# An encoder layer in three float32r products: the low parts of weights written by ACT and an adding DMA instead of a subtraction on DVE

## The chip, the cores and the metric

The kernel runs on one core of one Trainium2 chip. The metric is the device time of one launch in microseconds (us); the median of the runs is given. Engines are named as the profile names them: PE (TensorE), DVE (VectorE), ACT (ScalarE), POOL (GpSimd) and SP (SyncE, which here only issues DMAs).

## The reference

One layer of a bidirectional encoder is applied with the same weights to two requests: a prompt of 512 tokens and a sample of 1024 tokens, with 1024 channels, all in float32. Shortened to one request:

```python
def encoder_layer(x, c, ...):
    sh1, sc1, gt1, sh2, sc2, gt2 = split(silu(c) @ w_ada + b_ada, 6)
    h = rms_norm(x, g_pre_mix) * (1 + sc1) + sh1
    xa, ya, xb, ga, gb = split(h @ w_in)          # 1024, 1024, 512, 1024, 1024 columns
    xa = depthwise_conv(xa, conv_w, conv_b)       # width 4
    y_a = ((rg_lru(xa, forward) + rg_lru(xa, backward)) * gelu(ya)) @ w_a_out
    y_b = fourier_mix(xb) @ w_b_out               # 2-D DFT over positions and channels of a group
    x = x + gt1 * rms_norm((sigmoid(ga) * y_a + sigmoid(gb) * y_b) @ w_o, g_post_mix)
    h = rms_norm(x, g_pre_ffn) * (1 + sc2) + sh2
    val, gate = split(depthwise_conv(h @ w_up, ffn_conv_w, ffn_conv_b))   # 2816 and 2816, width 3
    return x + gt2 * rms_norm((gelu(gate) * val) @ w_down, g_post_ffn)

y_prompt = encoder_layer(x_prompt, c_prompt, ...)
y_sample = encoder_layer(x_sample, c_sample, ...)
```

## The kernel before

**Three products for one.** PE multiplies float32r, a rounded float32. Each float32 operand w is therefore split into a high part hi = float32r(w) and a low part lo = w − hi, and a product is the sum of hi·hi, hi·lo and lo·hi, added up in PSUM. The functions `passes`, `fm_mm` and `km_mm` issue them; all their matmuls have the line L200, and the transposes have L203.

**Units of weights.** The weights are worked off in units. A unit is one tile `raw` of 128 x 1024 float32, 512 KB, which `load_unit` loads by a DMA on SP's queue (L123; there are RAW_BUFS = 3 such tiles). `prep_unit` splits it into the two halves of a tile `hl` (HL_BUFS = 4 such tiles). There are three kinds of split. For a unit with `on_act`, ACT writes the high part (L108, a copy that rounds) and DVE subtracts it from the raw tile into the low part (L111). For a unit without `on_act`, DVE does both. A mixed unit (`mix`, the weights w_b of the Fourier branch) is first put together from sums and differences by DVE. 196 units have `on_act`: the sample's first projections (24, with 16 more for ya of both requests), w_a in the two merges (16), w_o and w_down (90), and the up projection where it is done plainly (50). The sample's up projection is mostly done by blocks (`up_quads`, seven block products in place of eight); its units have `whole=False`, and `prep_unit` isn't called for them.

**Steps and their order.** The program is one list of steps. A step has a unit, the products `mm` that use it, and what follows (`post`). `emit` goes through the list in order and, ahead of the products of step i, emits the splits of the units up to AHEAD = 3 further on, and the raw loads up to RAW_BUFS units beyond these; other loads of a step (`loads`) are emitted LOAD_AHEAD = 5 steps ahead. The instructions of an engine, and the DMAs of a queue, run in the order in which they were emitted. Only SP issues DMAs in this kernel. A function put off by `defer` is emitted one or more steps later.

**The stages**, with the times at which they stand in the profiled execution: the lead-in and the prompt's first projections (0 to 190 us), its Fourier branch and ya (to 280), the prompt merge (280 to 328), the prompt's w_o (to 373), the sample's first projections, Fourier branch and merge (to 960) and w_o (to 1030), the prompt's up projection (to 1297), the prompt's w_down (to 1425), the sample's up projection (to 1864) and the sample's w_down (to 2107), then the tail. Three of them matter for what follows:

- In the prompt merge (`merge_steps`), units of w_b (mixed, their products shorter) and of w_a (`on_act`, products yh x hl) take turns.
- In the prompt's w_down (`rows_steps`: 24 products a step), ACT also normalizes the sample's rows for the next sub-layer, one row of 128 tokens a step (`norm_rows`): a square with a sum (L412), two small operations on POOL for the reciprocal root (L429, L430, in `rstd`), and one step later the scaling (L417). The transposes of these rows (L203) follow from 1341.75 us on, between the weight steps.
- In the sample's w_down (`rows_steps` with `fsrc`), the activations f were stored to DRAM by the up projection (`fs`). In the first eleven of its steps, two tiles `fq` of 512 KB per step are read back on SP's queue (L1033), beside the raw weights, and are split into `ah` and `al` by ACT (L108) and DVE (L111) in `pre`, ahead of the step's weights.

Of the kernel before, what the change touches and what calls it, by code (L numbers as in the profile page):

```python
# [12 lines left out]
AF = mybir.ActivationFunctionType  # L13
ALU = mybir.AluOpType
PSUM = bass.MemoryType.PSUM
# [56 lines left out]
class Enc:  # L72
# [13 lines left out]

# [1 line left out]
    def nm(self, s):  # L88
# [14 lines left out]

# [1 line left out]
    def split(self, hi, lo, src, act=False, keep=None):  # L105
# [7 lines left out]
    def split_all(self, pairs):  # L113
        """Splits out of PSUM: one engine's reads of a bank before the other's."""
        nc = self.nc
        for out, src in pairs:
            nc.scalar.activation(out=out[:, 0, :], in_=src, func=AF.Copy)
        for out, src in pairs:
            nc.vector.tensor_tensor(out=out[:, 1, :], in0=src, in1=out[:, 0, :].bitcast(F32), op=ALU.subtract)
# [5 lines left out]
    def prep_unit(self, u):  # L125
        hl = self.sb.tile([128, 2, u.cols], F32R, tag="hl", bufs=HL_BUFS, name=self.nm("hl"))
        u.hi, u.lo = hl[:, 0, :], hl[:, 1, :]
        src = u.raw
        if u.mix:
            nc = self.nc  # L130
            src = self.big([128, u.cols], name="wb")
# [4 lines left out]
        if u.mix:  # L136
# [3 lines left out]
            return  # L140
        self.split(u.hi, u.lo, src, act=u.on_act)

# [1 line left out]
    def defer(self, fn, d):  # L144
# [52 lines left out]

# [1 line left out]
    def mmul(self, *args, **kw):  # L199
# [27 lines left out]
    def fm_chunks(self, sq, ps, f, mirror=False):  # L227
        """Output columns and the operand's; a mirrored operand has the later half of the tokens back to front."""
        n = sq.n
        cols = [slice(0, 512), slice(n, n // 2, -1) if mirror else slice(512, 1024)]  # L230
        return [(ps[:, f, c * 512:(c + 1) * 512], cols[c]) for c in range(sq.chunks)]
# [15 lines left out]

# [1 line left out]
    def setup(self):  # L249
# [71 lines left out]
    def ada_steps(self, job):  # L321
        """One part of the conditioning: a row of its weights per partition, two dot products with each."""
        nc = self.nc
# [53 lines left out]

# [1 line left out]
    def fold_loads(self):  # L379
# [25 lines left out]

# [1 line left out]
    def norm_rows(self, x, later):  # L407
# [81 lines left out]

# [1 line left out]
    def lead_in(self, sq, src, jobs, hb, sizes):  # L491
# [150 lines left out]

# [1 line left out]
    def conv_a(self, sq, ps, g, box):  # L644
# [150 lines left out]

# [1 line left out]
    def pq_steps(self, sq, hb, pq):  # L797
# [108 lines left out]

# [1 line left out]
    def merge_steps(self, sq, yb, z, sig, mg):  # L908
# [84 lines left out]

# [1 line left out]
    def rows_steps(self, sq, table, act, gate, src, dst, last=False, fsrc=None):  # L995
# [106 lines left out]

# [1 line left out]
    def quad_sums(self, hb):  # L1104
        """Sums of the activations' blocks (halves of the channels by halves of the tokens), in two parts as they are."""
        nc = self.nc
# [38 lines left out]
    def up_quads(self, sq, hb, dst, plain):  # L1145
        """The widest product by blocks, seven products of blocks for two tiles of columns."""
        nc = self.nc
# [3 lines left out]
        def finish(g, ca, cb):  # L1151
            """Convolution, gelu and product, a little at a time."""
            box = {}
# [278 lines left out]

# [1 line left out]
def _dft(n):  # L1434
# [105 lines left out]
```

## Time and profile before

| what | value |
|---|---|
| time, median of 3 runs | 2117.44 us (2117.34 to 2117.49) |
| span of the profiled execution, first to last instruction | 2115.4 us |
| PE busy | 2096.1 us, 99% |
| PE weight loads, beside the matmuls | 1721.6 us, 81% |
| DVE busy | 1424.4 us, 67% |
| ACT busy | 915.9 us, 43% |
| POOL busy | 55.0 us, 3%, 124 instructions |
| DMA | 274.66 MB, mean 130 GB/s; queue of SP 37.1% of the 16 engines' span |
| mean granted TensorE clock | 0.999 |

For the profiled execution the profile gives its span; the time of a run is taken around the whole launch, and the median lies 2.0 us above this span. Busy time is that of the engine's instructions; waiting and issuing are not in it. The stretches between the times above can be read apart, with the busy time of each engine in each of them.

### The profile page before, as it was taken

What the parts mean: (1) busy time and instruction counts of PE and PEld (TensorE: products, weight loads), DVE (VectorE), ACT (ScalarE), POOL (GpSimd) and SP (SyncE); (2) the same over time, 40 slices, a digit from 0 to 9 for tenths busy, and PEclk for the clock granted to TensorE, in tenths of its full rate; (3) what the DMA queues carried; (4) which work ended last, traced back from release to release, by engine and by line L of the source; (5) the groups of instructions that cost most, each with busy time, mean ns of one, the idle gap of its engine ahead of it and who ended that gap; (6) DMA issues with size and microseconds to landing.
All of it is one profiled execution on the core that took longest, in us unless ns stands there. A gap on an engine that the chain in (4) does not pass through costs nothing.

```text
span 2115.4 us, 24826 instructions
## 1 busy us (share of the span) xinstructions
PE 2096.1 (99%) x9866; PEld 1721.6 (81%) x9866; DVE 1424.4 (67%) x1815; ACT 915.9 (43%) x1199; POOL 55.0 (3%) x124
## 2 busy tenths in 40 slices
PE   7999999999999999999999999999999999999998
PEld 6888888888888988888888888888888888888887
DVE  5787888667666734655676545649688887875553
ACT  2447355265464422144433335633344444455442
POOL 0000010000000000000100000000000000000000
PEclk9999999999999999999999999999999999999999
DMA  9343474332332413433453224332122222284422
GB/s 350 114 149 130 180 269 162 113 109 85 110 105 65 141 50 108 141 141 135 175 186 112 99 99 156 113 130 90 50 80 80 90 72 82 96 315 163 149 91 109
DMA packets 90803, 274.66 MB, mean 130 GB/s; under 512 B 8736, under 2 KB 26560, under 8 KB 90688
## 3 DMA queue, kind: packets, MB, share of 16 engines
q1 hardware_dynamic: 90688, 273.09, 37.1%
q8 instruction: 77, 1.26, 0.2%
q14 instruction: 38, 0.31, 0.1%
HBM read 234.22 MB, written 38.83 MB: 129 GB/s over the span
## 4 chain that ended last, share of the span: by engine, by line
PE 95%; ACT 2%; DVE 1%; DMA 1%; issue 0%; POOL 0%; SPq 0%; DVEq 0%; POOLq 0%; ACTq 0%
PE ps L200 94%; PE ps L203 1%; DMA x<-in_x_prompt_dram 0%; ACT xn L412 0%; ACT th L685 0%; DVE hl L111 0%; DMA x<-in_x_sample_dram 0%; DVE yb L964 0%; ACT th L695 0%; ACT ea L693 0%; POOL sm L430 0%; DVE th L716 0%; DVE th L721 0%; ACT xn L417 0%; DVE th L719 0%
## 5 line engine op out<-in xcount | busy, mean ns | idle before, releaser
L200 PE MATMUL ps<-hh,hl 128*128 128x512 f32 x2144 | 633.8, 395 | 0.0
L200 PEld LDWEIGHTS ps<-hh,hl 128*128 128x128 f32 x2144 | 403.7, 188 | 95.2 <-DVE hl L111 0.2
L200 PE MATMUL ps<-hl,ah 128*128 128x512 f32 x1440 | 452.2, 395 | 0.0
L200 PE MATMUL ps<-hl,hl 128*128 128x512 f32 (+1 forms) x1264 | 436.2, 378 | 0.0
L111 DVE TENSOR_TENSOR hl<-raw,hl 128x1024 fp32r<-128x1024 f32 (+2 forms) x244 | 293.8, 1206 | 163.3 <-ACT hl L108 160.9
L200 PE MATMUL ps<-hx,wq 128*128 128x512 f32 x1596 | 370.9, 394 | 0.0
L200 PEld LDWEIGHTS ps<-hx,wq 128*128 128x128 f32 x1596 | 299.6, 188 | 71.1 <-DVE wq L1222 0.2
L108 ACT ACTIVATE hl<-raw 128x1024 fp32r<-128x1024 f32 x196 | 205.6, 1054 | 270.8 <-PE ps L200 243.4
L200 PEld LDWEIGHTS ps<-hl,ah 128*128 128x128 f32 x1440 | 269.1, 188 | 61.5
L200 PE MATMUL ps<-hl,al 128*128 128x512 f32 x720 | 283.8, 394 | 0.0
L200 PEld LDWEIGHTS ps<-hl,hl 128*128 128x128 f32 x1264 | 238.3, 189 | 47.5
L200 PEld LDWEIGHTS ps<-hl,al 128*128 128x128 f32 x720 | 135.2, 188 | 31.8
L1318 DVE SCALAR_TENSOR_TENSOR cf<-ps,vec,cf 128x511 f32<-128x511 f32 (+1 forms) x100 | 75.2, 807 | 83.8 <-ACT cf L1310 83.6
L200 PE MATMUL ps<-yh,hl 128*128 128x512 f32 x384 | 111.9, 394 | 0.3 <-DVE hl L111 0.3
L1166 DVE SCALAR_TENSOR_TENSOR cf<-cq,vec,cf 128x1023 f32<-128x1023 f32 x76 | 97.0, 1277 | 0.0
L1221 ACT ACTIVATE wq<-wsum 128x512 fp32r<-128x512 f32 x76 | 46.1, 629 | 117.7 <-DVE wsum L1232 117.7
L200 PEld LDWEIGHTS ps<-yh,hl 128*128 128x128 f32 x384 | 71.5, 188 | 16.9 <-DVE hl L111 0.7
L1310 ACT ACTIVATE cf<-ps,vec 128x512 f32<-128x512 f32 (+1 forms) x50 | 39.1, 826 | 105.9 <-PE ps L200 105.9
L111 DVE TENSOR_TENSOR al<-fq,ah 128x512 fp32r<-128x512 f32 x88 | 57.3, 687 | 32.3 <-PE ps L200 18.4
L738 ACT ACTIVATE sg<-ps 128x1024 f32<-128x1024 f32 x24 | 24.7, 1028 | 118.8 <-PE ps L200 118.7
L200 PE MATMUL ps<-hl,hh 128*128 128x258 f32 x384 | 69.2, 282 | 0.0
L659 DVE SCALAR_TENSOR_TENSOR xc<-ps,vec,xc 128x511 f32<-128x511 f32 (+3 forms) x48 | 46.9, 1012 | 30.1 <-ACT xc L651 29.5
(181 smaller groups left out, 2359.6 us busy)
## 6 DMA issues: line engine op xcount, KB each, us to landing
raw<-in_w_up_dram SPq DMA_DIRECT2D x88, 512.0 KB, 3.5
raw<-in_w_down_dram SPq DMA_DIRECT2D x66, 512.0 KB, 3.5
ada<-in_w_adaT_dram SPq DMA_DIRECT2D x32, 512.0 KB, 4.7
raw<-in_w_o_dram SPq DMA_DIRECT2D x24, 512.0 KB, 3.5
fs<-cf SPq DMA_DIRECT2D x22, 512.0 KB, 2.6
fq<-fs SPq DMA_DIRECT2D x22, 512.0 KB, 5.8
ada<-in_w_ada_dram SPq DMA_DIRECT2D x16, 512.0 KB, 8.9
raw<-in_w_gb_dram SPq DMA_DIRECT2D x16, 512.0 KB, 4.3
```

The source lines that it names most:

```text
L108: nc.scalar.activation(out=hi, in_=src, func=AF.Copy)
L111: nc.vector.tensor_tensor(out=lo, in0=src[:, 0:keep], in1=hi[:, 0:keep].bitcast(F32), op=ALU.subtract)
L200: self.nc.tensor.matmul(*args, **kw)
L203: self.nc.tensor.transpose(*args)
L659: nc.vector.scalar_tensor_tensor(out=xc[:, f, o], in0=ps[:, f, o.start + d:o.stop + d], scalar=w[:, tap:tap + 1], in1=xc[:, f, o], op0=ALU ...
L738: self.nc.scalar.activation(out=t, in_=ps, func=AF.Tanh, scale=0.5)
L1166: nc.vector.scalar_tensor_tensor(out=box[key][:, o], in0=c[:, i], scalar=self.vec[:, V_FW + 3 * m + t:V_FW + 3 * m + t + 1], in1=box[key][ ...
L1221: nc.scalar.activation(out=hi, in_=src, func=AF.Copy)
L1310: nc.scalar.activation(out=acc[:, f, :], in_=ps[:, f, :], func=AF.Identity, scale=w[:, 1:2], bias=self.vec[:, V_FB + m:V_FB + m + 1])
L1318: nc.vector.scalar_tensor_tensor(out=acc[:, f, o], in0=ps[:, f, o.start + d:o.stop + d], scalar=w[:, tap:tap + 1], in1=acc[:, f, o], op0=A ...
```

## The change

In `prep_unit`, a unit with `on_act` isn't split by `split` any more. ACT writes the high part as before (L142 of the changed kernel) and then, with the same function and scale −1, float32r(−w) into the low part's place (L143). Then POOL issues a DMA with an adding write (L144): it reads the raw tile and the place, adds, and writes raw − hi there. The subtraction on DVE goes. The low part is now there when this DMA has landed, and the raw tile comes free then. Units without `on_act`, mixed units, the activations' splits and the block products stay as they are. The rest of the diff takes out comments; lines behind it stand 5 higher (L1033 becomes L1038).

```diff
     def prep_unit(self, u):
...
-        self.split(u.hi, u.lo, src, act=u.on_act)
+        if u.on_act:
+            self.nc.scalar.activation(out=u.hi, in_=src, func=AF.Copy)
+            self.nc.scalar.activation(out=u.lo, in_=src, func=AF.Copy, scale=-1.0)
+            self.nc.gpsimd.dma_start(out=u.lo, in_=src, accum_op=ALU.add)
+            return
+        self.split(u.hi, u.lo, src)
```

The order of ACT in the prompt's w_down, before: a row's square and the scaling, an activation's high part (`ah`), a unit's high part (`hl`), and the next row. (The number behind a name counts tiles; the one behind the underscore is the instruction's own.)

```order
L412 ACTIVATE xn1342_9802,sm1340_9800<-x1310_9660 128x1024
L417 ACTIVATE xn1342_9802<-x1310_9660,sm1341_9801 128x1024
L108 ACTIVATE ah1345_9834<-cf1258_9141 128x1024
L108 ACTIVATE hl1347_9838<-raw1319_9710 128x1024
L412 ACTIVATE xn1351_9845,sm1349_9843<-x1324_9719 128x1024
L417 ACTIVATE xn1351_9845<-x1324_9719,sm1350_9844 128x1024
```

ACT at the same place in the changed kernel:

```order
L417 ACTIVATE xn1342_9932,sm1340_9930<-x1310_9786 128x1024
L422 ACTIVATE xn1342_9932<-x1310_9786,sm1341_9931 128x1024
L108 ACTIVATE ah1345_9964<-cf1258_9252 128x1024
L142 ACTIVATE hl1347_9968<-raw1319_9838 128x1024
L143 ACTIVATE hl1347_9968<-raw1319_9838 128x1024
L417 ACTIVATE xn1351_9976,sm1349_9974<-x1324_9847 128x1024
```

One more write of 128 x 1024 stands between the unit's high part and the next row's square, in every step with such a unit.

The order of SP's DMAs at the start of the sample's w_down, with what each waits for, before: two tiles of `fq` and one of `raw` per step.

```order
L1033 DMA fq1823_13642<-fs_110 128x1024 [waits DMAHW3_49]
L1033 DMA fq1824_13644<-fs_110 128x1024 [waits DMAHW4_49]
L123 DMA raw1828_13655<-in_w_down_dram 128x1024 [waits DMAHW5_49,DVE_49]
L1033 DMA fq1829_13672<-fs_110 128x1024 [waits DMAHW6_49]
L1033 DMA fq1830_13674<-fs_110 128x1024 [waits DMAHW7_49,PE_49]
L123 DMA raw1834_13685<-in_w_down_dram 128x1024 [waits DMAHW0_49,DVE_49]
```

SP at the same place in the changed kernel:

```order
L1038 DMA fq1823_13794<-fs_110 128x1024 [waits DMAHW3_49]
L1038 DMA fq1824_13796<-fs_110 128x1024 [waits DMAHW4_49]
L123 DMA raw1828_13808<-in_w_down_dram 128x1024 [waits DMAHW5_49,DMASW0_49,Activation_49]
L1038 DMA fq1829_13825<-fs_110 128x1024 [waits DMAHW6_49]
L1038 DMA fq1830_13827<-fs_110 128x1024 [waits DMAHW7_49,PE_49]
L123 DMA raw1834_13839<-in_w_down_dram 128x1024 [waits DMAHW0_49,DMASW1_49,Activation_49]
```

The order is the same. A load of `raw` waited for DVE, whose subtraction read the tile last; it now waits for ACT and for a DMA of POOL's queue (DMASW), and the loads of `fq` of the next step stand behind it.

## Rows read from the trace of the kernel before

**Rows 1.** The page, part 1, busy us and shares of all engines.

```profile
PE 2096.1 (99%) x9866; PEld 1721.6 (81%) x9866; DVE 1424.4 (67%) x1815; ACT 915.9 (43%) x1199; POOL 55.0 (3%) x124
```

**Rows 2.** Busy time by stretch: PE, PEld, DVE, ACT, POOL, clock, DMA share, GB/s.

```profile
280.00:330.00 50.00, 49.57 (x267) 42.08 (x266) 43.83 (x62) 27.16 (x34) 7.39 (x12) 1.00 0.70 244
1020.00:1297.00 277.00, 277.00 (x1195) 224.04 (x1194) 165.38 (x204) 100.83 (x126) 5.46 (x12) 1.00 0.38 130
1297.00:1342.00 45.00, 45.00 (x197) 36.48 (x197) 22.84 (x22) 34.21 (x43) 8.88 (x16) 1.00 0.49 175
1846.00:1907.00 61.00, 61.00 (x265) 49.42 (x264) 43.89 (x53) 31.63 (x42) 0.00 (x0) 1.00 0.85 310
1907.00:2107.00 200.00, 200.00 (x864) 161.96 (x863) 100.24 (x123) 81.31 (x132) 6.74 (x20) 1.00 0.35 124
```

**Rows 3.** The critical chain in order of time: start us, us, what.

```profile
1341.75 0.87 PE ps L203 x8
...
1349.08 5.57 PE ps L200 x24
```

**Rows 4.** Groups by line and form: busy us, mean ns, idle before.

```profile
L111 DVE TENSOR_TENSOR hl<-raw,hl 128x1024 fp32r<-128x1024 f32 x218 | 266.0, 1222 | 162.4 <-ACT hl L108 160.9 <-DMA fq<-fs 0.3
...
L430 POOL TENSOR_TENSOR sm<-sm,mhalf 128x1 f32<-128x1 f32 x24 | 15.4, 640 | 2.0
```

**Rows 5.** The page, part 5, ACT writing the high parts of weights.

```profile
L108 ACT ACTIVATE hl<-raw 128x1024 fp32r<-128x1024 f32 x196 | 205.6, 1054 | 270.8 <-PE ps L200 243.4
```

**Rows 6.** ACT, timeline of the prompt w_down stage: start us, us, what.

```profile
1299.56 1.05 ACT L108 ACTIVATE hl<-raw 128x1024 fp32r<-128x1024 f32 x1
1300.51 1.05 ACT L412 ACTIVATE xn<-x 128x1024 f32<-128x1024 f32 x1
...
1337.58 1.04 ACT L108 ACTIVATE hl<-raw 128x1024 fp32r<-128x1024 f32 x1
...
1340.79 1.15 ACT L417 ACTIVATE xn<-x,sm 128x1024 f32<-128x1024 f32 x1 [1.12 <-POOL sm L430]
```

**Rows 7.** DMA issues by tensor: KB each, median us from issue to landing.

```profile
raw<-in_w_down_dram SPq DMA_DIRECT2D x66, 512.0 KB, 3.5
...
fs<-cf SPq DMA_DIRECT2D x22, 512.0 KB, 2.6
fq<-fs SPq DMA_DIRECT2D x22, 512.0 KB, 5.8
```

**Rows 8.** DMA queue in 1846 to 1907 us: packets, MB, share of 16 engines.

```profile
q1 hardware_dynamic: 5180, 18.86, 85.1%
```

**Rows 9.** ACT, timeline of the prompt merge: high parts of w_a.

```profile
281.92 1.06 ACT L108 ACTIVATE hl<-raw 128x1024 fp32r<-128x1024 f32 x1 [5.09 <-PE ps L200]
...
298.64 1.04 ACT L108 ACTIVATE hl<-raw 128x1024 fp32r<-128x1024 f32 x1
...
313.55 1.06 ACT L108 ACTIVATE hl<-raw 128x1024 fp32r<-128x1024 f32 x1 [3.63 <-DVE wb L135]
```

**Rows 10.** PE, timeline: the product that first reads the low part, same units.

```profile
287.17 0.63 PE L200 MATMUL ps<-yh,hl 128*128 128x512 f32 x2
...
301.47 0.63 PE L200 MATMUL ps<-yh,hl 128*128 128x512 f32 x2
...
316.73 0.61 PE L200 MATMUL ps<-yh,hl 128*128 128x512 f32 x2
```

**Rows 11.** ACT writing tile hl by stretch: busy us and, behind x, instructions.

```profile
1020.00:1297.00 277.00, 50.59 (x49) 1.00 0.38 130
...
1907.00:2107.00 200.00, 36.00 (x34) 1.00 0.35 124
...
280.00:330.00 50.00, 9.49 (x9) 1.00 0.70 244
```

**Rows 12.** ACT, timeline of the sample w_down stage, tenth unit.

```profile
1905.93 1.05 ACT L108 ACTIVATE hl<-raw 128x1024 fp32r<-128x1024 f32 x1
```

**Rows 13.** PE, timeline of the sample w_down stage, first unit.

```profile
1864.02 0.62 PE L200 MATMUL ps<-hl,ah 128*128 128x512 f32 x2
```

## The prediction, made before the changed kernel was run

> **What bounds the kernel now.** I read the page's busy shares first: PE is busy 99% of the span, 2096.1 of 2115.4 us, DVE 67%, ACT 43%, POOL 3% [rows 1]. Then busy time by stretch: in four of the five stretches shown PE never stops, in the fifth it idles 0.4 us, and the granted clock is 1.00 in all [rows 2]. The reader is to see that PE has next to no idle time to win back in the middle of the program: over the whole span it idles 2115.4 − 2096.1 = 19.3 us, in these five stretches of 633 us only 0.4 of it, and I put the rest at the start and the tail, where loads and the last norm are waited for. A DVE at 67% is not what ends anything. So relieving DVE is worth a microsecond at most, and the question is only whether the new path for the low part reaches PE in time. The profiled span is 2115.4 us, the median of the runs 2117.44; I add differences to the median.
>
> The beat: one weight unit of 24 products takes PE 5.57 us [rows 3], and a unit's buffer comes free when the unit four before it is done, so splitting one has three steps, 16.7 us, where steps are that long.
>
> **The change, part by part.**
>
> Removed: 196 subtractions on DVE at 1.22 us (the 218 of this form less 22 units that DVE splits alone) [rows 4], 239 us of DVE. On the path: about nothing, PE idles tenths at most where it reads low parts [rows 2].
>
> Added on ACT: 196 writes of the negated part. The nearest row is the high part, same tile and function, 1.05 us long [rows 5]; starts of neighbours stand 0.95 us apart (1299.56 to 1300.51 [rows 6]), so 0.95 us each, 186 us. Where ACT has idle time this is hidden.
>
> Added: 196 transfers of 512 KB on POOL's queue, in which the raw tile and the low part are read and the low part written. No row shows one. Lower end: a store, 2.6 us from issue to landing [rows 7]. Upper end: fq, a transfer in the fullest stretch, 5.8 us [rows 7], with another 2.2 us for a slow issue on POOL and for queueing, 8.0 us. I take 5.5: a weight load, 3.5 us [rows 7], plus 1.5 us for the second read, plus 0.5 us until POOL has issued, near POOL's own small operations of 0.64 us [rows 4]. The time it holds the 16 DMA engines: in the fullest stretch 18.86 MB took 85.1% of 61 us, 51.9 us for 36 transfers of this size, 1.44 us each [rows 8]. With two reads I take 3.0 us; ends 1.5 (as a copy) and 4.5.
>
> The Trainium skill, "DMA: Bandwidth & Descriptors", section "Anatomy of one DMA — SWDGE (gpsimd) path", puts a transfer issued from GpSimd at 2.0 us plus its bytes over 436 GB/s, which for 512 KB is 3.2 us, an estimate from that page. By it, with the bytes counted once (1.2 us of the engines), terms 2 to 4 below would be 4, 4 and 0 us and the time 2132. No run here shows such a transfer. "Collectives: The Full Stack" of the Trainium skill, section "The bandwidth ceiling: the fold count and why AG ≠ RS ≠ AR", says that a reduction by DMA reads two sources on one ring and ran at half the rate of a copy; by that the doubled engine time stands, and so does my sum.
>
> Now the places where the cover is thin.
>
> 1. The prompt w_down stage, ACT itself. Between 1297 and 1342 us ACT takes one unit and one row of norms per PE step: 43 instructions, and 34.2 of 45 us busy [rows 2], the rest mostly waits for POOL inside the norm. The period is (1337.58 − 1299.56) / 7 = 5.43 us [rows 6] against PE's 5.57. With 0.95 us more it is 6.4: ACT falls behind. Eight high parts from 1299.56 to 1337.58 come before the last normalized row, which is done at 1340.79 + 1.15 = 1341.94 [rows 6]; PE starts to transpose at 1341.75 and needs this row last of eight, about 0.6 us later [rows 3]. So 8 × 0.95 = 7.6, less 0.6: **7 us**, whatever the transfer costs. Ends: 7, and 13 if POOL's issue, which stands ahead of the norm's POOL steps, takes 2 us and holds them up by 0.8 each.
>
> 2. The prompt merge, 280 to 330 us. Steps of w_b are short, so a w_a unit that follows two of them has little lead. Its high part starts at 281.92, 298.64 and 313.55 [rows 9]; PE first reads the low part at 287.17, 301.47 and 316.73 [rows 10]. The new low part is there 1.9 + 5.5 = 7.4 us after the start: late by 2.2, 4.6 and 4.2 us, 11 us in all. Counted by engines: share 0.70 of 50 us [rows 2] and nine transfers [rows 11] of 3.0 make 62, 12 us too much. Both are the same stall; I take **12**. Ends: 3 (2.6 us and a copy's engine time: late by 0, 1.7, 1.3) and 25 (4.5 us of the engines).
>
> 3. The sample w_down stage, 1846 to 1907 us. Here fq is read back beside the weights and the engines are 85% busy [rows 8]. SP's load of the raw tile waits until the tile three before it has been used, now by the transfer, and the fq loads stand behind it in SP's queue; ACT's fq split, high part and negation stand behind those. The stage's 11 units add 11 × 3.0 = 33 us of transfers where 61 − 51.9 = 9.1 us are free: 24 us late. Lead that could absorb it: the tenth unit's high part starts at 1905.93 [rows 12], its low part is read at 1864.02 + 9 × 5.57 + 0.23 = 1914.4 [rows 13]; of these 8.5 us the new path uses 7.4. So **24 us**, less about 1 that I neglect. Ends: 7 (1.5 us each) and 40 (4.5).
>
> 4. Elsewhere: 49 transfers in 1020 to 1297 us, 34 in 1907 to 2107 [rows 11], with engine shares of 0.38 and 0.35 [rows 2]. 49 × 3.0 / 277 = 0.53, 34 × 3.0 / 200 = 0.51: together 0.91 and 0.86. That holds on average, but loads and transfers now queue behind each other and the raw tile is held longer: landing 5.5 and the next load 3.5 stand in one ring of three tiles with ACT's 1.9, 10.9 of 16.7 us. I allow **10 us**, a choice; ends 0 and, at 4.5 us, 0.38 × 277 + 220 − 277 = 49 plus 0.35 × 200 + 153 − 200 = 23.
>
> The long steps of the sample mixer (48 products, twice the lead) and the quad products, which the diff leaves alone, cost nothing. POOL's 196 issues fit beside 55 us of work.
>
> Sum: 7 + 12 + 24 + 10 = 53; 2117.4 + 53 = **2170 us**, slower by 2.5%. 0.2%, 4.2 us, is what a measurement of this kernel can tell from no change.
>
> **The rivals.**
>
> Light transfer: it holds the engines like a copy, 1.5 us, and lands in 2.6 to 3.5 us. Then 7 + 3 + 7 + 0 = 17, 2135 us; with a little queueing up to 2150, and 2130 if the units' lead absorbs most of term 3. For it: stores land in 2.6 us [rows 7]. Against: three passes over SBUF instead of two. The page of the Trainium skill on bandwidth, named above, would bring the time here; what it leaves out is the second read.
>
> Heavy transfer: 4.5 us of the engines or more. Then the transfers become the bound of every stretch with 24-product steps, since 1.44 + 4.5 exceeds 5.57: 7 + 25 + 40 + 49 + 23 = 144, 2261 us; at 6.0 us the same working gives 7 + 39 + 57 + 122 + 74 = 299, 2416 us. For it: nothing shows how fast an adding transfer runs. Against: half-rate reads explain 3.0 already.
>
> Not slower: the low part lands nearly as soon as DVE's subtraction did, within about 2 us, and ACT's norm chain is relieved as much as it is loaded, since ACT idles 1.12 us at POOL in each row of norms [rows 6] and an earlier entry into this stretch could use up the 7 us. Then 2117 to 2121 us. It decides at a landing of 2 us and term 1 below 4.2. Against: ACT's queue is in order, so that idle time can't be filled; and 2.6 us is the fastest landing of any 512 KB transfer shown.
>
> That the change doesn't do what it says is excluded by the order of the built program: 196 DMA rows on POOL, 196 more writes on ACT, 196 subtractions fewer on DVE.
>
> **How the numbers follow.** Forecast (engine time 2.4 to 3.6, 2150 to 2205 us): 0.53. Light: 0.23. Heavy: 0.16. Not slower: 0.08, of it 0.01 faster, since there is hardly a microsecond to gain. The range takes in the light case and the mild third of the heavy one, 0.53 + 0.23 + 0.05 = 0.81: 2130 to 2290. Slower by over 0.2%: 0.92; within: 0.07; faster: 0.01.
>
> **What would show it.** DVE's busy time falls by about 239 us, ACT's rises by 186 to 206, a second DMA queue moves some 103 MB. PE's idle time rises from 19 to about 70 us, and its waits name the transfer into hl, in the merge and in the first eleven units of the sample w_down, and ACT's normalized rows at the first transposes near 1342. PE's own group means stay. Wrong would be: no wait at the transposes (term 1), a landing well under or over 5.5 us, or waits spread over all stages (heavy).

## The result, and the profile after

The changed kernel takes 2178.64 us (median of 4 runs, 2175.07 to 2187.4), the one before 2117.47 us (4 runs, 2117.34 to 2117.82): slower, ratio 1.0294, 95% interval 1.0273 to 1.0315. The medians lie 61.2 us apart. The profiled execution has a span of 2178.3 us against 2115.4 us, 62.9 us more; the stages below are read from it.

The page of the changed kernel, part 1 (busy us and shares), which answers to [rows 1]:

```profile
PE 2114.6 (97%) x9866; PEld 1731.3 (79%) x9866; DVE 1201.3 (55%) x1619; ACT 1098.5 (50%) x1395; POOL 218.1 (10%) x320
```

DVE lost 223 us of work and ACT gained 183. POOL's 218.1 us hold 171.6 us of its 196 issues, which the page counts as busy in this kernel. PE's idle time went from 19.3 to 63.7 us, 44.4 more, and its busy time rose by 18.5 us for the same 9866 matmuls. The two make the 62.9 us.

Parts 3 and 6 of the page, queues (packets, MB, share of 16 engines) and DMA issues (KB each, median us to landing), to be read beside [rows 7]:

```profile
q1 hardware_dynamic: 90688, 273.09, 36.6%
q0 software_dynamic: 28224, 102.77, 25.4%
...
hl<-raw POOLq DMA_DIRECT2D x196, 512.0 KB, 5.8
...
raw<-in_w_down_dram SPq DMA_DIRECT2D x66, 512.0 KB, 5.2
...
fq<-fs SPq DMA_DIRECT2D x22, 512.0 KB, 7.0
```

The additions move 102.77 MB and hold the 16 engines 25.4% of the span, 0.254 × 2178.3 / 196 = 2.82 us each. They land after 5.8 us in the median; loads of w_down now take 5.2 us instead of 3.5, and fq 7.0 instead of 5.8. All instructions of line L144, with the shortest, median and longest:

```profile
L144 POOL DMA_DIRECT2D hl<-raw x196: 852/871/1214, 210.1 to 2152.0; - x196
...
DMA to landing us min/median/max: 4.4/5.8/11.1
```

POOL is held 0.87 us by each issue, and no addition landed sooner than 4.4 us after it.

Where PE waits, from its timeline (start, us, what, and in brackets the wait just before and its releaser), all waits over 2.3 us from the merge on:

```profile
283.18 1.22 PE L205 MATMUL ps<-yh,hl 128*128 128x512 f32 x2 [6.42 <-DMA hl<-raw]
...
303.44 1.22 PE L205 MATMUL ps<-yh,hl 128*128 128x512 f32 x2 [5.53 <-DMA hl<-raw]
...
1371.87 0.48 PE L208 MATMUL ps<-ident,xn 128*128 128x128 f32 x1 [5.91 <-ACT xn L422]
...
1910.98 0.49 PE L205 MATMUL ps<-hl,ah 128*128 128x512 f32 x1 [2.41 <-DMA hl<-raw]
...
1927.86 0.50 PE L205 MATMUL ps<-hl,ah 128*128 128x512 f32 x1 [3.88 <-DMA hl<-raw]
...
1944.73 0.51 PE L205 MATMUL ps<-hl,ah 128*128 128x512 f32 x1 [3.82 <-DMA hl<-raw]
...
1954.95 0.50 PE L205 MATMUL ps<-hl,ah 128*128 128x512 f32 x1 [2.81 <-DMA hl<-raw]
...
1968.03 0.79 PE L205 MATMUL ps<-hl,ah 128*128 128x512 f32 x1 [5.68 <-DMA hl<-raw]
```

The waits stand in three places: the prompt's merge, the first transposes in the prompt's w_down (ACT's normalized row), and the first eleven steps of the sample's w_down. The smaller ones beside them are 2.21 and 0.43 us in the merge (and 0.41 us there for DVE), 0.77 us at the transposes, 0.96 us in the sample's w_down, and elsewhere one of 0.89 us at 258 us and one of 2.22 us at 1125 us.

The busy time that PE gained is the clock: the mean time of a product rose in the groups of these three places (yh x hl from 394 to 403 ns, hl x ah from 395 to 402), while hh x hl, which has none of these waits, stayed at 395. Busy time around the first wait in the merge, columns as in [rows 2]; the last three figures of a row are granted clock, DMA share and GB/s:

```profile
281.00:283.00 2.00, 0.00 (x0) 0.00 (x0) 1.45 (x7) 1.15 (x2) 0.19 (x1) 0.50 0.24 45
283.00:287.00 4.00, 3.82 (x9) 3.05 (x10) 0.90 (x3) 1.15 (x1) 0.56 (x1) 0.50 0.68 234
287.00:290.00 3.00, 3.00 (x14) 2.39 (x14) 1.47 (x3) 1.64 (x3) 0.74 (x2) 0.98 0.98 358
```

PE did nothing from 276.76 to 283.18 us. The granted clock fell to 0.50 (1.2 GHz) meanwhile and stayed there until about 287 us, so 9 products took 3.82 us where 14 took 3.00 right behind.

By stage, from PE's first and last products of each (us):

| stage | before | after | more | forecast |
|---|---|---|---|---|
| prompt's merge (yh x hl) | 58.5 | 77.5 | 19.0 | 12 |
| from its end to the first transposes | 1014.0 | 1016.0 | 2.0 | elsewhere |
| first transposes to the sample's w_down | 522.4 | 531.6 | 9.2 | 7 |
| sample's w_down | 245.1 | 276.0 | 30.9 | 24 |
| ahead of the merge, and the tail | 275.3 | 277.1 | 1.8 | elsewhere |
| sum | 2115.4 | 2178.3 | 62.9 | 53, of it 10 elsewhere |

### The profile page after: what moved, and what is told of

The parts are those of the page before. It is cut to its first block, busy times and chain, and to the rows that moved or that the text cites. A ratio compares the mean times of both kernels' runs of the same rounds, so it can differ in the third digit from the quotient of the medians.

```text
span 2178.3 us, 25496 instructions
## 1 busy us (share of the span) xinstructions
PE 2114.6 (97%) x9866; PEld 1731.3 (79%) x9866; DVE 1201.3 (55%) x1619; ACT 1098.5 (50%) x1395; POOL 218.1 (10%) x320
## 3 DMA queue, kind: packets, MB, share of 16 engines
q0 software_dynamic: 28224, 102.77, 25.4%
## 4 chain that ended last, share of the span: by engine, by line
PE 81%; DMA 7%; issue 6%; ACT 3%; DVE 2%; POOL 1%; SPq 0%; POOLq 0%; DVEq 0%; ACTq 0%
PE ps L205 80%; DMA hl<-raw 4%; PE ps L208 1%; DMA raw<-in_w_up_dram 1%; DMA raw<-in_w_a_dram 1%; DMA raw<-in_w_o_dram 1%; ACT hl L143 1%; ACT hl L142 1%; DMA ada<-in_w_adaT_dram 0%; ACT ah L108 0%; POOL hl L144 0%; DMA raw<-in_w_ya_dram 0%; DMA x<-in_x_prompt_dram 0%; DMA raw<-in_w_down_dram 0%; POOL sm L435 0%
## 5 line engine op out<-in xcount | busy, mean ns | idle before, releaser
L205 PE MATMUL ps<-hl,ah 128*128 128x512 f32 x1440 | 463.0, 402 | 19.8 <-DMA hl<-raw 19.8
L144 POOL DMA_DIRECT2D hl<-raw x196 | 171.6, 876 | 1860.8 <-ACT hl L143 1325.2
L205 PEld LDWEIGHTS ps<-hl,ah 128*128 128x128 f32 x1440 | 274.3, 192 | 87.2 <-DMA hl<-raw 23.8
L142 ACT ACTIVATE hl<-raw 128x1024 fp32r<-128x1024 f32 x196 | 206.5, 1054 | 251.7 <-PE ps L205 110.3
L143 ACT ACTIVATE hl<-raw 128x1024 fp32r<-128x1024 f32 x196 | 204.7, 1044 | 0.0
L205 PE MATMUL ps<-yh,hl 128*128 128x512 f32 x384 | 115.0, 403 | 15.0 <-DMA hl<-raw 14.6
L1064 DVE TENSOR_TENSOR ro<-ps,gate 128x512 f32<-128x512 f32 x48 | 31.1, 687 | 97.9 <-ACT junk L1056 97.9
L108 ACT ACTIVATE ah<-fq 128x512 fp32r<-128x512 f32 x88 | 51.0, 619 | 48.2 <-DMA fq<-fs 48.2
```

Of the source, the lines that this page charges most:

```text
L108: nc.scalar.activation(out=hi, in_=src, func=AF.Copy)
L142: self.nc.scalar.activation(out=u.hi, in_=src, func=AF.Copy)
L143: self.nc.scalar.activation(out=u.lo, in_=src, func=AF.Copy, scale=-1.0)
L144: self.nc.gpsimd.dma_start(out=u.lo, in_=src, accum_op=ALU.add)
L205: self.nc.tensor.matmul(*args, **kw)
L1064: nc.vector.tensor_tensor(out=rows[o][:, cols], in0=p, in1=gate["gate"][:, cols], op=ALU.mult)
```

## The experiments

Each was timed beside the kernel before on the same chip. Diffs are against the changed kernel. The length of a stage comes from one profiled execution of each kernel. Run 9 leaves the merge as it is in the changed kernel and has it at 79.3 us, where the changed kernel has 77.5; runs 6 and 10 leave the sample's w_down as it is and have it at 278.1 and 272.0 us, where the changed kernel has 276.0. So a difference of 2 us in the merge, or of 4 us in the sample's w_down, tells nothing.

**1. The negation on DVE.**

```diff
-            self.nc.scalar.activation(out=u.lo, in_=src, func=AF.Copy, scale=-1.0)
+            self.nc.vector.tensor_scalar(out=u.lo, in0=src, scalar1=-1.0, scalar2=None, op0=ALU.mult)
```

> The negated raw tile is written by DVE instead of ACT; the adding DMA stays. Theory: the loss has three separate places, and the one at the first transposes of the prompt's w_down (PE idle 6.67 us there, and 6.83 us at a clock of 0.5 right behind it, worth 3.4 us) is ACT's own, so it goes, and the merge and the sample's w_down keep theirs: about 2168 us (2160 to 2174). Rival: all of it is the DMA's engine time, the wait at the transposes included; then no change, 2176 to 2181 us.

Measured: 2192.49 us, ratio 1.0346 (1.0327 to 1.0365). Both expectations fell: it is slower than the changed kernel. In the profiled execution, the fastest of the four, the sample's w_down takes 281.5 us, 5.5 more; why the other three take 6 to 10 us more was not seen. With ACT relieved of 182 us, the wait at the transposes is still there, 1.24 and 5.87 us:

```profile
1366.17 0.33 PE L208 MATMUL ps<-ident,xn 128*128 128x128 f32 x1 [1.24 <-ACT xn L422]
1372.37 0.48 PE L208 MATMUL ps<-ident,xn 128*128 128x128 f32 x1 [5.87 <-ACT xn L422]
```

Two rows of ACT's timeline, 6.21 us apart:

```profile
1333.88 1.16 ACT L422 ACTIVATE xn<-x,sm 128x1024 f32<-128x1024 f32 x1 [2.11 <-POOL sm L435]
...
1340.09 1.15 ACT L422 ACTIVATE xn<-x,sm 128x1024 f32<-128x1024 f32 x1 [2.12 <-POOL sm L435]
```

And POOL's timeline ahead of the second:

```profile
1338.26 0.90 POOL L144 DMA_DIRECT2D hl<-raw  x1 [4.41 <-DVE hl L143]
1339.24 0.18 POOL L434 TENSOR_SCALAR sm<-sm 128x1 f32<-128x1 f32 x1
1339.50 0.56 POOL L435 TENSOR_TENSOR sm<-sm,mhalf 128x1 f32<-128x1 f32 x1
```

POOL issues the addition only when DVE has the negated part, and the norm's two operations stand behind the issue. What ACT saved it now waits for POOL: 2.12 us a row against 1.12 before the change [rows 6]. This is not quite the changed kernel's own case: DVE writes the negated part behind its subtraction for `al`, so POOL issues at 1338.26, when ACT's square (1336.84 to 1337.89) is over. In the changed kernel POOL issues beside the square, and ACT waits 1.21 us for it.

**2. The negation without the DMA.**

```diff
-            self.nc.gpsimd.dma_start(out=u.lo, in_=src, accum_op=ALU.add)
+            self.nc.vector.tensor_tensor(out=u.lo, in0=src, in1=u.hi.bitcast(F32), op=ALU.subtract)
```

> ACT still writes the negated raw tile, but DVE then subtracts as before the change and overwrites it; no adding DMA. Theory: only ACT's term is left, one wait of 6 to 7 us at the first transposes of the prompt's w_down, and up to 3.4 us of lower clock behind it: about 2126 us (2122 to 2130). Rival (the transfers are the whole cause): 2117 to 2119 us.

Measured: 2127.21 us, ratio 1.0042 (1.0027 to 1.0057), as the theory had it. One wait is left:

```profile
1349.69 0.47 PE L208 MATMUL ps<-ident,xn 128*128 128x128 f32 x1 [5.64 <-ACT xn L422]
```

ACT's period per row is 5.98 us here:

```profile
1330.57 1.15 ACT L422 ACTIVATE xn<-x,sm 128x1024 f32<-128x1024 f32 x1 [0.94 <-POOL sm L435]
...
1336.55 1.15 ACT L422 ACTIVATE xn<-x,sm 128x1024 f32<-128x1024 f32 x1 [0.94 <-POOL sm L435]
```

It was 5.21 before the change (1335.58 to 1340.79 in the same lines) and is 6.25 with it, in the changed kernel's own lines:

```profile
1339.40 1.16 ACT L422 ACTIVATE xn<-x,sm 128x1024 f32<-128x1024 f32 x1 [1.21 <-POOL sm L435]
...
1345.65 1.16 ACT L422 ACTIVATE xn<-x,sm 128x1024 f32<-128x1024 f32 x1 [1.22 <-POOL sm L435]
```

So ACT's extra write alone gives most of this wait, 0.77 us of the 1.04 us that a row became longer; POOL's issue adds 0.27. Run 1 had 7.1 us of waits without the extra write, from POOL's later issue. With ACT's write and POOL's issue both, the changed kernel waits 6.67 us, not the sum. Merge (59.5 us) and sample's w_down (244.8 us) are within 1 us of those before the change: there the loss needs the transfers.

**3. A copy instead of the addition.**

```diff
-            self.nc.gpsimd.dma_start(out=u.lo, in_=src, accum_op=ALU.add)
+            self.nc.gpsimd.dma_start(out=u.lo, in_=src)
```

> The same DMA from POOL without the addition: it copies raw over the negated tile. This leaves out the subtraction of the high part, so the low part is the whole weight; sizes, order and waits are as in the change. Theory: the second read is what makes the transfer hold the engines 2.8 us (25.4% of 2178.3 us over 196) instead of some 1.4; without it the waits in the sample's w_down fall from 19.6 to about 7 us, those in the merge from 14.6 to about 5, the lower clock with them, and the transposes keep their 6.7: about 2145 us (2135 to 2158). Rival (what costs is the path over POOL's queue and the landing, not the addition): 2168 us or more.

Measured: 2156.41 us, ratio 1.018 (1.0165 to 1.0196), at the upper end of what the theory gave. The page of this run, the same two lines:

```profile
q0 software_dynamic: 28224, 102.77, 13.2%
...
hl<-raw POOLq DMA_DIRECT2D x196, 512.0 KB, 3.5
```

A copy holds the engines 0.132 × 2155.8 / 196 = 1.45 us and lands in 3.5 us: the addition costs twice the engine time for the same bytes written, and 2.3 us more to land. The copy's issue is shorter too, it holds POOL 0.53 us in the median. But the waits fell less than expected, to 13.9 us in the sample's w_down and 6.3 in the merge (expected 7 and 5). With copies a step there needs 3 × 1.44 + 1.45 = 5.8 us of transfers, 0.2 over PE's 5.57, which would make some 2 us in eleven steps. So the engines' time is not the only limit. The row of this stretch shows it:

```profile
1882.90:1966.00 83.10, 69.15 (x269) 53.80 (x268) 24.68 (x32) 41.49 (x54) 6.36 (x13) 0.92 0.82 278
```

The engines are busy to 0.82 here, less than the 0.85 before the change [rows 2], where PE never waited.

**4. Low parts used last.** `fm_mm` and `km_mm` issue all products with the high part of the weight first:

```diff
-        for k in range(nk):
-            for q, (w, x) in enumerate(self.passes(u, xh, xl)):
+        order = [(k, q) for k in range(nk) for q in range(2)] + [(k, 2) for k in range(nk)]
+        for k, q in order:
+            w, x = self.passes(u, xh, xl)[q]
```

> The change, and in each unit the products that read the low part of the weight go behind the other sixteen, which gives the low part 16 x 0.232 = 3.7 us more lead. Theory: in the merge the waits are a matter of lead and fall from 6.4, 5.5 and 2.2 to about 2.7, 1.8 and 0 us; in the sample's w_down the DMA engines are short of time (two fq at 1.44, one raw at 1.44 and 2.8 for the addition make 7.1 us per step of 5.57), so the lead is used up once and the sum falls only from 19.6 to about 16; transposes unchanged: about 2163 us (2155 to 2170). Rival (lead everywhere): each wait there loses up to 3.7 us too, the sum falls to about 3, and the lower clock goes: 2135 to 2145 us.

Measured: 2171.9 us, ratio 1.0246 (1.022 to 1.0272), outside both. In the sample's w_down the waits sum to 15.6 us, as the theory had it (16), and the stage takes 269.4 us; 8.0 of the 15.6 us are now waits for ACT's high part, which no later use of the low part can cover. In the merge the waits for additions fell from 14.6 to 9.0 us, but the merge takes 77.0 us instead of 77.5: other waits took their place. More lead for the low part alone gains nothing there.

**5. The old split in three places.** 30 units go back to ACT and DVE.

```diff
-        if u.on_act:
+        if u.on_act and not u.dve:
...
+            u.dve = sq.nf == 2 and table is self.a["w_a"]
...
+                    u.dve = table is self.a["w_down"] and t0 == 0 and half == 0
```

> The change, but 30 of the 196 units are split as before it: the 8 units of w_a in the prompt's merge, the first 11 of the prompt's w_down and the first 11 of the sample's w_down. Theory: the loss is made in these three stretches alone, where the cover is thin; the other 166 transfers cost the two short waits seen elsewhere (0.9 and 2.2 us), and relieving DVE by 203 us gains nothing: 2117 to 2123 us, and the clock at 1.00 from 42 us to the end. Rival (the transfers load the DMA engines everywhere, and the waits move to the next thin place): 2130 us or more.

Measured: 2122.79 us (10 runs, 2119.65 to 2126.45), ratio 1.0024 (1.0014 to 1.0033). The profiled execution, the fastest of these, has a span of 2117.9 us:

```profile
PE 2096.9 (99%) x9866; PEld 1721.2 (81%) x9866; DVE 1234.8 (58%) x1649; ACT 1070.4 (51%) x1365; POOL 195.8 (9%) x290
```

166 additions are still there and cost 4.8 us. So some 56 of the 61 us were made by 30 units in three places. And DVE with 190 us less to do gives nothing back: the kernel is not faster than before. Where the other runs lost up to 7 us more than the profiled one was not seen.

**6. PE's waits in the merge filled with work.**

```diff
         nk = len(xh)
+        for _ in range(u.fill):     # 24, 20 and 8 in w_a's units 1, 2 and 4
+            for out, cols in outs:
+                self.mmul(out, lhsT=u.hi[:, col0:col0 + 128], rhs=xh[0][:, cols], start=True, stop=True)
```

> The change, and in three units of w_a in the prompt's merge PE repeats the unit's first product 24, 20 and 8 times ahead of it (each restarts the sum, so nothing is added), which fills most of the waits of 6.42, 5.53 and 2.21 us with work; the low parts come no sooner. Theory: the two stretches at a clock of 0.5 behind these waits go, each worth 3.4 us, and nothing else changes: the merge, from 276.4 us to the end of its last product, gets 6 to 7 us shorter, the time about 2172 us. Rival (the lower clock is not the idle time's doing): the clock is still 0.5 there and the merge as long as in the change or longer.

Measured: 2181.82 us, ratio 1.0298 (1.0281 to 1.0316): not shorter. The merge as one stretch, of the change and of this run:

```profile
270.50:348.00 77.50, 62.50 (x301) 51.32 (x301) 43.89 (x81) 44.25 (x57) 15.14 (x25) 0.91 0.87 262
```

```profile
270.00:347.70 77.70, 71.89 (x353) 59.48 (x352) 43.91 (x81) 44.85 (x58) 15.00 (x25) 0.98 0.89 266
```

The mean clock rose from 0.91 to 0.98, so the lower clock was the idle time's doing, but the merge takes 77.7 us as it took 77.5. What PE does faster here it waits for longer: the chain that sets the merge's end runs over PE for 27 of its 74 us only. The critical chain of the changed kernel shows it:

```profile
274.05 9.09 DMA hl<-raw
...
284.59 7.43 DMA raw<-in_w_a_dram
292.12 1.06 ACT hl L142
...
294.54 8.85 DMA hl<-raw
303.44 16.01 PE ps L205 x72
```

An addition lands after 9 us, only then SP loads the next raw tile (7.4 us), ACT splits it (2 us), and the next addition follows; then PE works for 16.0 us. The second stretch on PE is the 11.0 us from 337.09 us to the merge's end.

**7. Four raw tiles.**

```diff
-RAW_BUFS = 3
+RAW_BUFS = 4
```

> The change with four raw tiles instead of three, so that a load need not wait for the landing of the addition three units back but for that four back. Theory: in the first eleven steps of the sample's w_down the DMA engines are short of time (7.1 us of transfers per step of 5.57), so a fourth tile brings a unit of lead once, and the waits there fall from 19.6 to no less than 10 us; the merge, with engines busy to 0.91, gains 2 to 6; transposes unchanged: 2158 to 2172 us. Rival (the ring of three tiles is the limit, the engines have room): the waits of both places fall below 5 us in all, 2128 to 2140 us.

Measured: 2167.58 us, ratio 1.0237 (1.0222 to 1.0252), inside the theory's range. The waits in the sample's w_down sum to 16.8 us, in run 12, which also has four tiles, to 20.3; with three tiles it was 19.6 in the changed kernel and 18.0 in run 10. The merge takes 74.5 us, little more than the scatter below 77.5. The ring alone is not the limit in either place. (The expectation puts the engines' share in the merge at 0.91; in the changed kernel's row under 6 it is 0.87, and 0.91 is the clock.)

**8. POOL's issue behind the norm**, with the negation on DVE as in 1:

```diff
+            def add(u=u, src=src):
+                self.nc.gpsimd.dma_start(out=u.lo, in_=src, accum_op=ALU.add)
+            if u.dly:               # the first 11 units of the prompt's w_down
+                self.defer(add, 1)
+            else:
+                add()
```

> The negation on DVE as in the run before, and in the first 11 units of the prompt's w_down POOL issues the addition one step later, behind the two small operations of the next row's norm instead of ahead of them. Theory: the wait at the transposes that stayed when ACT was relieved was POOL's: its issue (0.89 us) and its wait for the negated part stood ahead of the norm's operations, and ACT waited 2.12 us for them in each row against 1.12 before the change; now ACT's period falls from 6.21 to about 5.2 to 5.4 us, the wait at the transposes from 7.1 to under 1 us, with the clock at 1.00 behind it: about 10 us less than with the negation on DVE alone, some 2182 us. Rival (late raw tiles or the transfer hold ACT): period and wait stay, 2190 us or more.

Measured: 2188.63 us, ratio 1.033 (1.0313 to 1.0347); run 1 had 2192.49, so 4 of the expected 10 us came. ACT's timeline:

```profile
1331.81 1.15 ACT L428 ACTIVATE xn<-x,sm 128x1024 f32<-128x1024 f32 x1 [2.90 <-POOL sm L441]
...
1336.86 1.16 ACT L428 ACTIVATE xn<-x,sm 128x1024 f32<-128x1024 f32 x1 [0.96 <-POOL sm L441]
...
1340.96 1.06 ACT L143 ACTIVATE hl<-raw 128x1024 fp32r<-128x1024 f32 x1 [2.00 <-DMA raw<-in_w_down_dram]
...
1344.02 1.15 ACT L428 ACTIVATE xn<-x,sm 128x1024 f32<-128x1024 f32 x1 [0.96 <-POOL sm L441]
```

The wait for POOL is gone (0.96 us), and the period is 5.05 us (1331.81 to 1336.86) where nothing else is late. The wait at the transposes falls from 7.1 to 2.59 us, not under 1, because a third cause shows: in the next row ACT waits 2.00 us for the raw tile, whose load is late. This run makes that cause greater itself, since an addition that is issued later holds its raw tile longer.

**9. One tile of fq for all.**

```diff
                             def f():
+                                if k:
+                                    act[k] = act[0]
+                                    return
                                 act[k] = self.big([128, 1, 1024], name="fq")
```

> The change, with one of the 22 tiles of fq loaded and used for all 22, which leaves out 21 loads (the sample's output is computed from the first tile of f alone). The path of the low part, the rings and the order stay. Theory: in the first eleven steps of the sample's w_down the time of the DMA engines is the limit; without two fq loads a step needs 4.3 us of transfers per 5.57 us of PE, so PE's waits there fall from 19.6 to under 3 us, the clock stays at 1.00, the stage falls from 276.0 to 245 to 249 us, the time to 2146 to 2156 us. Rival (the landing and the ring of raw tiles are the limit): waits of over 10 us stay, 2165 us or more.

Measured: 2146.35 us, ratio 1.0128 (1.0111 to 1.0145). The sample's w_down takes 245.5 us, as before the change (245.1), with one wait of 0.33 us:

```profile
1896.00:1985.00 89.00, 88.67 (x383) 71.53 (x383) 34.06 (x49) 58.12 (x80) 16.16 (x22) 1.00 0.92 224
```

All 31 us of this stage come from additions and fq loads together; the landing and the ring of three tiles, which are still there, cost nothing without fq. The row also warns: the engines are busy to 0.92 and PE never waits, so a high DMA share alone proves no limit. Nor does a queue that waits. This is SP in the changed kernel and in this run, from 1896 to 1985 us (us in total, times, longest):

```profile
SPq L123 <- DMA hl<-raw: 71.4, 11, 11.8
```

```profile
SPq L123 <- DMA hl<-raw: 86.8, 19, 9.0
```

SP waits for landings even longer here, and PE is not held up. The run leaves one thing unseparated. Without fq the engines have less to do, but the fq loads are also gone from SP's queue, where they stood behind loads of raw that wait for a landing.

**10. One x tile beside the merge.**

```diff
             def f():
+                if t and sub == 0 and sq.idx == 1:
+                    rows.append(rows[0])
+                    return
                 x = self.big([128, 1024], name="x")
```

> The change, with one of the eight x tiles of the sample loaded ahead of the prompt's merge and used for all eight rows of the first norm, which leaves out seven loads of 512 KB beside the merge (the sample's first normalization then sees the first 128 tokens only). Theory: in the merge too the engines' time is the limit, which would be why filling PE's waits did not shorten it; 7 x 1.44 = 10 us less makes the merge, 77.5 us, 8 to 11 us shorter: 2166 to 2172 us. Rival (the low parts are late by their own path): merge within 2 us of 77.5.

Measured: 2178.77 us, ratio 1.0284 (1.0267 to 1.0301). The merge takes 81.2 us, not less, though the DMA share fell:

```profile
271.60:352.80 81.20, 63.62 (x301) 51.90 (x300) 43.90 (x81) 42.96 (x56) 15.83 (x25) 0.89 0.77 208
```

The theory fell: in the merge the engines' time alone is not the limit. Why the merge came out longer was not seen.

**11. Run 2 with the wait at the transposes filled.**

```diff
-                    for t in range(sq.tt):
+                    for t in list(range(sq.tt - 1)) * (7 if quads and g == 0 else 1) + [sq.tt - 1]:
```

> ACT writes the negated part and DVE subtracts, no adding DMA, and ahead of the first transposes in the prompt's w_down the seven rows that are there are transposed six times more than needed (42 x 0.13 = 5.5 us), which fills the wait of 5.63 us. Theory: here no transfer limits what follows, so the lower clock behind the wait did cost time, 3.3 us at 0.5 = 1.7 us; it goes, and the stretch from the first transpose to the sample's w_down falls from 530.2 to about 528.4 us. Rival (the lower clock costs nothing here either): 530 us or more.

Measured: 2125.16 us against 2127.21 in run 2. From the first transpose (1344.39) to the sample's w_down (1872.85) it takes 528.5 us instead of 530.2, and the clock is 1.00 throughout. Here PE is the bound behind the wait, and the lower clock did cost its 1.7 us.

**12. Four raw tiles and one x tile.** The edits of 7 and 10 together.

> A fourth raw tile and only one of the sample's eight x tiles loaded beside the merge (the sample's first normalization sees the first 128 tokens only). Alone the tile took 3 us off the merge and the missing loads none. Theory: two limits lie close together there, the ring of raw tiles, whose loads stood 62 us of the stretch from 255 to 345 us behind landings of the addition, and the time of the engines, 0.87 busy; with both loosened the merge falls from 77.5 to 62 to 69 us. Rival (it is neither, but the lead was lost ahead of the merge, or in another queue): 73 us or more.

Measured: 2167.38 us, ratio 1.0232 (1.0215 to 1.0252). The merge takes 70.2 us, between the two expectations: less than with either edit alone (74.5 and 81.2), but not free. A part of what is left has the length of the path itself, as in this pair from ACT's and PE's timelines:

```profile
281.53 1.06 ACT L142 ACTIVATE hl<-raw 128x1024 fp32r<-128x1024 f32 x1 [3.06 <-PE ps L205]
```

```profile
288.51 0.73 PE L205 MATMUL ps<-yh,hl 128*128 128x512 f32 x2 [1.20 <-DMA hl<-raw]
```

ACT could start only when PE had given a tile of `hl` back, and the low part was there 7.0 us later.

## Why the prediction was right, and where it was not

**The bound: right.** PE was the bound, and DVE's 223 us are worth nothing: with 190 us off DVE and the three bad places avoided, run 5 is 4.8 us slower than before, not faster.

**The prices: right in the median, too low where it counted.** Taken were 5.5 us to landing and 3.0 us of the engines; measured 5.8 and 2.82 over the program. But the nine additions issued between 270 and 348 us landed after 7.4 us in the median, the nine between 1895 and 1968 us after 7.7. DVE's busy time fell by 223 us and not by 239, since the prediction took each subtraction's whole 1.22 us, though neighbours on an engine overlap at their ends, as it did allow for on ACT. The step from a load's 1.44 us to twice that by a second read is what run 3 shows (1.45 against 2.82). Of the two rules of the Trainium skill, the one in "Collectives: The Full Stack", section "The bandwidth ceiling: the fold count and why AG ≠ RS ≠ AR" (two sources on one ring, half the rate), is told there of reductions between cores; this pair agrees with it. The one in "DMA: Bandwidth & Descriptors", section "Anatomy of one DMA — SWDGE (gpsimd) path", gives 3.2 us for 512 KB, an estimate from that page: near the 3.5 us of the copy in run 3, but the addition takes 5.8, and 2132 us was far off.

**Term 1, the transposes: 7 us, measured 9.2.** The wait is 6.67 us, nearly the forecast's size, and most of the rest is the lower clock behind it: 0.50 until about 1376 us, 4 us into the work, worth some 2 us (an estimate from these rows; the expectation of run 1 took 6.83 and 3.4 us). The prediction put the wait on ACT, "whatever the transfer costs", and run 2 bears that out: 5.64 us without any adding transfer. The prediction's period of 5.43 us averages in a first row of 6.75; the later rows were 5.21 us apart before the change. It saw POOL's issue as something that would be added, up to 13 us. In the changed kernel the issue adds 0.27 us a row, because POOL issues while ACT writes the next row's square; issued after the square, as in run 1, it made a row 1.00 us longer by itself. Late raw tiles, the third cause, show in run 8 alone.

**Term 2, the merge: 12 us, measured 19.0.** Of the 19.0 us, 14.6 are waits for additions, near the 12, but not where the prediction counted them. It counted the third, fifth and seventh unit of w_a [rows 9], 2.2, 4.6 and 4.2 us late; measured were 5.53, 2.21 and 0.43 us. The longest wait, 6.42 us, is at the second unit (1 in run 6, which counts from 0), which had lead enough before, 9.3 us from its high part to the first use of its low part. These are ACT's writes of its high part, before the change and with it:

```profile
265.76 1.04 ACT L108 ACTIVATE hl<-raw 128x1024 fp32r<-128x1024 f32 x1
```

```profile
271.65 1.04 ACT L142 ACTIVATE hl<-raw 128x1024 fp32r<-128x1024 f32 x1
```

The merge's first product came only 1.5 us later than before, this write 5.9 us later: 4.4 us of lead were lost ahead of the merge. The critical chain follows the write back to loads of the conditioning weights (`ada`), which land after 8.0 us in the median between 200 and 270 us, against 4.7 before the change. And from this write to the landing it took 11.5 us (271.65 to 283.14), in the third unit 11.3, where the prediction had 7.4. So the places and the price of the path were wrong in part, and that the sum came near is luck. The step that failed beside it is "Both are the same stall". They are not: the time of the engines (run 10), the lead (run 4) and PE's clock (run 6) can each be loosened without making the merge any shorter, the ring by hardly more than the scatter (run 7), and ring and engines together take 7.3 us off (run 12); a transfer that is shorter in both ways takes 9.1 off (run 3, a merge of 68.4 us). In the chain under 6 a longer path closes on itself: raw tile, split, addition, next raw tile. The prediction counted how late one low part is and not that the next load starts from its landing. How the 19 us divide between this path, the ring of `hl` and the lead lost ahead of the merge stays open.

**Term 3, the sample's w_down: 24 us, measured 30.9.** The idle time is 19.6 us of it, and PE works some 11 us longer at the lower clock. That fq and the additions make it together is shown (run 9); that it is the engines' time, as the sum had it, is not: run 3 halves that time and keeps 13.9 us of waits, run 7 widens the ring and keeps 16.8. The changed kernel's trace shows a path that closes on itself here too. PE goes on with the seventh unit at 1944.73 us, when its addition lands. The same landing frees the raw tile for the tenth unit's load, and only behind that load SP issues the fq loads of the ninth:

```profile
1944.74 0.33 SPq L123 DMA_DIRECT2D raw<-in_w_down_dram  x1
1945.16 0.86 SPq L1038 DMA_DIRECT2D fq<-fs  x2
```

ACT has to split these fq ahead of the ninth unit's weights, and POOL issues the ninth addition behind that:

```profile
1955.09 0.63 ACT L108 ACTIVATE ah<-fq 128x512 fp32r<-128x512 f32 x1 [3.30 <-DMA fq<-fs]
...
1958.02 0.86 POOL L144 DMA_DIRECT2D hl<-raw  x1 [12.26 <-ACT hl L143]
```

It lands at 1968.03 us, after PE has waited 5.68 us: 23.3 us from landing to landing for two units that PE works off in 11.1. The prediction told this path in words, and then summed the engines' time alone. The order of SP's queue ties a unit to the landing two units before it, and the transfers in the path are slow in this stretch, where the engines are busy to 0.88: about 9.5 us for the second fq, 10.0 for the addition. How much is order and how much engines no run separated, since none took fq out of SP's queue and kept its bytes.

**Term 4, elsewhere: 10 us, measured 3.8.** The allowance was too large. The up projection with 49 additions shows one wait of 2.2 us.

**What the sum left out is the clock.** The prediction expected that the mean times of PE's products stay. 53 us were forecast, 62.9 came, of them 44.4 idle. The forecast counted idle time alone and was 9 us too high for that; 18.5 us are PE's slower work behind the waits, which no term had. So the total came close because an allowance and an omission partly cancelled, which is luck. Not every one of the 18.5 us is a loss of its own: at the transposes it is (run 11), in the merge it is not (run 6). The rivals fell by their own marks: the engine time is neither 1.5 nor 4.5 us.

## What to carry to other kernels

Before an engine is relieved, look whether anything ends on it: 223 us off an engine that is busy 67% gave back nothing here. A result that is made by a DMA instead of an instruction turned a 1.2 us step into one of 5.8 us in the median and of up to 11.1 here, and its source tile is held as long, so the places to look at are those where a tile has little lead, where a queue in order stands behind that tile, and where the issuing engine has small operations that others wait for. Ask also what a late landing holds up that then makes the next landing late: a price per transfer misses a path that closes on itself. When several queues wait on one another, as at the transposes here, price the slowest of them and not their sum, and expect the next one to show when the first is taken away.

## What the runs showed that was not expected

- The granted clock fell to 0.50 (1.2 GHz) in PE's longer waits and stayed there for a few us of work: behind the wait of 6.42 us until about 287 us, 4 us into the work, and behind the one of 5.64 us in run 2 until about 1353 us, 3.3 us into the work. Behind the wait of 2.41 us it fell only when PE had been at work again for about 1 us; behind those of 2.21 and 2.22 us it stayed at 1.00. In the whole changed program PE's same work took 18.5 us longer.
- The lower clock was free in the merge, where transfers set most of the pace (run 6), and cost its full share at the transposes, where PE does (run 11).
- An adding transfer of 512 KB in SBUF holds the engines 2.82 us, a copy of the same shape 1.45 us. Its issue holds POOL 0.87 us, the copy's 0.53 us, and the small operations behind it wait that long.
- Kernels with additions scatter more: the changed kernel by 12.3 us over 4 runs and run 5 by 6.8 us over 10, the kernel before by 3.0 us over 13 beside run 5.
